# The scan's backward chain dealt out over the steps on GpSimd, and both norm-weight rows spread ahead of the transposes

## The chip, the cores and the metric

The kernel runs on one core of a Trainium2 chip. A core has TensorE (matmuls, PE in the profile; its weight loads are listed as PEld), VectorE (DVE), ScalarE (ACT), GpSimd (POOL) and SyncE (SP). The engines run side by side, each through its own queue of instructions in a fixed order, and wait for each other by semaphores. DMA transfers are issued here from the queues of SP and ACT. The metric is the device time of one execution in microseconds (us).

## What is computed

The reference is one layer of a hybrid encoder on a sequence of 1024 tokens with 1024 channels. Cut to what matters here:

```
h = rmsnorm(x, norm_mix)
proj = h @ w_in                       # q, k, v, z, x/B/C, dt and gates
ssd:  x, B, C = silu(conv(xbc));  dt = softplus(dt_raw + bias)
      y = scan_forward(x, dt, B, C) + scan_backward(x, dt, B, C) + d_skip * x
      y = group_rmsnorm(y * silu(z))
merged = gate_a * (attention @ w_a) + gate_b * (ssd @ w_s)
x = x + merged @ w_out;  x = x + cross_attention(rmsnorm(x), rmsnorm(mem));  x = x + mlp(rmsnorm(x))
```

Both scans go by chunks of 128 tokens, eight in all. Within a chunk a product with a masked decay matrix gives the local part; between chunks a state is carried along: `state[c+1] = decay[c] * state[c] + contribution[c]` forward, and the same from the last chunk to the first backward. The output of chunk c adds `C` times the states that enter the chunk from either side.

## The kernel before

Matmuls of the big projections are done as three products of split numbers (high by high, high by low, low by high), which is why weights are split after loading: ScalarE copies the high part (L66), GpSimd subtracts it for the low part (L69, tile `wlo`).

**The start (`phase0`).** Two 128-row tiles of `mem` and eight of `x` are normalised. Their norm weights come as one row each (`gr`), and TensorE spreads a row over 128 partitions by products with a column of ones into PSUM (tile `gb`, two halves of 512 columns, L225 and L228). `norm_rows` takes the sum of squares on ScalarE (L131), the power on GpSimd (L124) and scales on VectorE (L143). `mem_split` transposes a tile on TensorE (L191, tile `nt`) and copies it to `mT` on ScalarE (L192). In the order of TensorE, the row for `mem` is spread first, then the first tile of `mem` is transposed, then one half of the row for `x` is spread, then the second tile is transposed, then the other half. After that come the key and value products of `mem` (`kx_unit`, L203, tile `kxp`; `vx_unit`), alternating with the transposes of the `x` tiles.

**The scan (`ssd_phase`).** Channels form eight groups. TensorE works through jobs that are written out by hand, in which every unit is three matmuls: for a group two convolution jobs (`conv_job`), a gate job, two more convolution jobs and a job for `z`. Between units, small pieces of the scan are put at given places: the eight `state` pieces of a group lie in its `z` job, and the eight `step` pieces of the group before lie in the first four jobs of the next, from step 7 down to step 0, two in a job of 16 units.

- `state(q, c)` makes the contribution of chunk c (TensorE, tile `st`), carries the forward state on VectorE (L511, L512) and puts the contribution to the backward state into `prev[:, c-1, 1]` by ScalarE (L514).
- `back(q)` carries the backward state on GpSimd: six links from chunk 6 down to 1, each a product with the decay into a tile `cb_t` (L520) and an addition into `prev[:, c-1, 1]` (L521). Before, it is called once, at the end of the group's `z` job. `cb_t` shares the two buffers `p1` with a tile of the steps.
- `prep(q, c)` loads cumulative decays for chunk c (`rows`, two DMAs issued on ACT's queue, L528), GpSimd masks them (L529 and L531, the triangle of either direction), ScalarE takes eight exponentials (L538, L539, tiles `ef` and `eb`), and VectorE adds the two (L540).
- `mask(q, c)` multiplies `ef` with the product of B and C (L545 on TensorE, L547 on VectorE).
- `step(q, c)` calls `mask` for chunk c-1 and `prep` for chunk c-2, then does the local products (L561, into `cb`) and the product of C with the entering states `prev[:, c]` (L565, tile `yo`). VectorE scales `yo` into `t` (L569). GpSimd makes the skip term `p1` (shown as `p`, L573) and adds the backward part of `t` (L575). VectorE sums up into `yz` (L577 to L579), ScalarE squares (L580).
- `conv_post` follows a convolution job: a first pass on ScalarE (L379), four on VectorE (L383, L385), a tanh (L387) and a last one on VectorE (L388).

TensorE's order is that of the program. The other engines' orders, and the slots of buffers, are made at build time by a list scheduler, which goes by the place of an instruction in the program and by its own estimate of when the inputs are there. A piece can so be moved ahead of its place: `prep`'s loads and masks run up to three steps early where the buffers allow it. `tc.issue_after(ins)` keeps what is traced inside it behind `ins` on the engine of `ins`.

## Time and profile before

| | |
|---|---|
| median of 3 runs | 2375.82 us (2375.48 to 2376.95) |
| profiled execution | 2374.8 us, its span 2373.0 us |
| TensorE busy | 2328.3 us (98%) |
| VectorE busy | 1567.7 us (66%) |
| ScalarE busy | 1124.2 us (47%) |
| GpSimd busy | 865.4 us (36%), 827 instructions |
| scan, by the steps | about 151 to 935 us of the span |

A row of the timeline gives the start and the length in us, the engine, the line, the operation, the output and input tiles with their shapes, how many instructions are merged in the row, and in brackets how long the engine was idle before and what ended that. "ACTq" is a queue of DMA issues. A row of waits gives who waited for whom, the total in us, how many times, and the longest. A row of one line's instructions gives minimum, median and maximum in nanoseconds and the first and last start. In the row of a stretch stand its bounds, its length and the busy time and count of PE, PEld, DVE, ACT and POOL, then the granted clock, the DMA share and the data rate.

### The profile page before, as it was taken

How to read it: one execution, taken by the hardware profiler on the slowest of the kernel's cores; microseconds unless marked ns; L12 is line 12 of the kernel's file. 1: busy time of each engine (PE TensorE's matmuls, PEld its weight loads, DVE VectorE, ACT ScalarE, POOL GpSimd, SP SyncE). 2: the span in 40 equal slices, each digit the busy share in tenths (PEclk: the TensorE clock that was granted, in tenths of full speed). 3: DMA queues.
4: the chain of work that ended last, by engine and by line, in shares of the span. 5: the costliest groups of instructions: out<-in, count | busy, mean ns of one | idle time of the engine just before them, and what ended most of it. 6: DMA issues, size and time to landing. Idle time of an engine off the chain costs nothing.

```text
span 2373.0 us, 32192 instructions
## 1 busy us (share of the span) xinstructions
PE 2328.3 (98%) x11812; PEld 1930.2 (81%) x11812; DVE 1567.7 (66%) x2523; ACT 1124.2 (47%) x2398; POOL 865.4 (36%) x827
## 2 busy tenths in 40 slices
PE   9999999999999999999999999999999999999998
PEld 7888888888888887877777888888987887788887
DVE  4757566565756654375658987975685456689984
ACT  4445545555554555387765543345543333234341
POOL 2244536263443625255541013305475444200010
PEclk9999999999999999999999999999999999999999
DMA  6223323232322323111116247203253345722301
GB/s 219 84 77 98 87 83 115 72 107 68 111 78 92 107 75 104 45 36 54 39 52 228 101 151 266 89 1 98 98 173 125 110 135 175 281 94 77 128 27 71
DMA packets 150033, 251.01 MB, mean 106 GB/s; under 512 B 11250, under 2 KB 86130, under 8 KB 149876
## 3 DMA queue, kind: packets, MB, share of 16 engines
q1 hardware_dynamic: 79264, 210.67, 26.3%
q10 hardware_dynamic: 70612, 38.29, 5.7%
q8 instruction: 93, 1.52, 0.3%
q14 instruction: 64, 0.52, 0.1%
HBM read 201.47 MB, written 47.45 MB: 105 GB/s over the span
## 4 chain that ended last, share of the span: by engine, by line
PE 70%; DVE 12%; POOL 7%; ACT 5%; issue 4%; DMA 2%; POOLq 0%; ACTq 0%; SPq 0%; DVEq 0%
PE dps L1482 10%; PE mps L1482 8%; PE pb L1277 5%; PE pc L1277 3%; PE zp L89 3%; PE zp L85 2%; PE zp L90 2%; PE cps L90 2%; PE cps L85 2%; PE cps L89 2%; PE st L506 2%; POOL prev L521 2%; DVE cx L385 1%; PE mps L85 1%; POOL cb_t L520 1%
## 5 line engine op out<-in xcount | busy, mean ns | idle before, releaser
L69 POOL TENSOR_TENSOR wlo<-raw,whi 128x1024 fp32r<-128x1024 f32 x104 | 255.0, 2453 | 471.9 <-ACT whi L66 459.1
L1433 ACT ACTIVATE kt<-row 128x512 fp32r<-128x512 f32 x264 | 144.0, 620 | 185.8 <-PE dps L1482 83.2
L1482 PE MATMUL mps<-kt 128*128 128x512 f32 x1008 | 230.5, 390 | 1.5 <-DVE kt L1434 1.5
L1482 PE MATMUL dps<-kt 128*128 128x512 f32 x1008 | 228.6, 389 | 0.0
L1482 PEld LDWEIGHTS mps<-kt 128*128 128x128 f32 x1008 | 188.7, 188 | 42.1 <-DVE kt L1434 3.1
L1482 PEld LDWEIGHTS dps<-kt 128*128 128x128 f32 x1008 | 189.2, 188 | 39.3
L85 PE MATMUL cps<-kt,whi 128*128 128x512 f32 x512 | 215.0, 420 | 0.0
L66 ACT ACTIVATE whi<-raw 128x1024 fp32r<-128x1024 f32 x104 | 109.6, 1055 | 203.5 <-DMA raw<-in_wa_dram 42.7
L90 PE MATMUL cps<-kt,wlo 128*128 128x512 f32 x512 | 200.0, 391 | 0.0
L89 PE MATMUL cps<-kt,whi 128*128 128x512 f32 x512 | 199.4, 389 | 0.0
L1434 DVE TENSOR_TENSOR kt<-row,kt 128x512 fp32r<-128x512 f32 x264 | 171.9, 698 | 4.1 <-ACT kt L1433 4.0
L124 POOL TENSOR_TENSOR rr<-rv,mhalf 128x1 f32<-128x1 f32 (+1 forms) x50 | 35.0, 701 | 239.4 <-DVE rv L122 237.6
L529 POOL TENSOR_SCALAR_AFFINE_SELECT rows<-rows 128x512 f32<-128x512 f32 x64 | 44.2, 691 | 202.5 <-DMA rows<-d_cs 201.6
L1223 POOL TENSOR_TENSOR wop<-w,wop 128x512 fp32r<-128x512 f32 x64 | 86.0, 1347 | 85.8 <-ACT wop L1222 79.9
L89 PEld LDWEIGHTS cps<-kt,whi 128*128 128x128 f32 x512 | 96.3, 188 | 25.4 <-issue 6.7
L85 PEld LDWEIGHTS cps<-kt,whi 128*128 128x128 f32 x512 | 96.2, 188 | 25.1 <-issue 6.7
L90 PEld LDWEIGHTS cps<-kt,wlo 128*128 128x128 f32 x512 | 96.1, 188 | 20.7
L85 PE MATMUL gps<-kt,whi 128*128 128x512 f32 x240 | 102.2, 426 | 0.0
L539 ACT ACTIVATE eb<-rows,ebias 128x128 f32<-128x128 f32 x256 | 89.1, 392 | 23.3 <-POOL rows L531 23.3
L719 DVE CUSTOM_DVE_ANT_0 t<-sps,bias 128x384 f32<-128x384 f32 (+1 forms) x128 | 64.4, 522 | 51.6 <-PE sps L718 49.6
L730 POOL TENSOR_SCALAR t<-t,den 128x384 f32<-128x384 f32 (+1 forms) x128 | 69.2, 560 | 80.3 <-DVE den L728 70.8
L538 ACT ACTIVATE ef<-rows,ebias 128x128 f32<-128x128 f32 x256 | 90.1, 391 | 14.7 <-PE cb L561 14.7
(372 smaller groups left out, 6387.6 us busy)
## 6 DMA issues: line engine op xcount, KB each, us to landing
rows<-d_cs ACTq DMA_DIRECT2D x128, 256.0 KB, 3.8
raw<-in_wssd_dram SPq DMA_DIRECT2D x48, 512.0 KB, 3.6
raw<-in_wup_dram SPq DMA_DIRECT2D x40, 512.0 KB, 3.8
d_u<-c SPq DMA_DIRECT2D x64, 256.0 KB, 2.6
row<-in_wdn_dram SPq DMA_DIRECT2D x28, 512.0 KB, 6.6
row<-d_u SPq DMA_DIRECT2D x28, 512.0 KB, 6.6
x<-in_x_dram SPq DMA_DIRECT2D x16, 512.0 KB, 6.2
raw<-in_wg_dram SPq DMA_DIRECT2D x16, 512.0 KB, 3.5
```

The costliest lines, as they stand in the source:

```text
L66: steps = [nc.scalar.activation(hi, raw, AF.Copy)]
L69: steps.append((eng or nc.gpsimd).tensor_tensor(lo, raw, hi.bitcast(F32), ALU.subtract))
L85: i = mm(out, l[0], r[0], start=first, stop=False)
L89: mm(out, l[0], r[1], start=False, stop=False)
L90: mm(out, l[1], r[0], start=False, stop=last)
L538: A.activation(ef[:, h], rows[:, 0, h], AF.Exp, bias=kx.ebias[:, b, j, 0, o:o + 1])
L539: A.activation(eb[:, h], rows[:, 1, h], AF.Exp, bias=kx.ebias[:, b, j, 1, o:o + 1])
L1223: self.kx.nc.gpsimd.tensor_tensor(t[:, 1], src, t[:, 0].bitcast(F32), ALU.subtract)
L1277: self.kx.nc.tensor.matmul(ps, w[:, i, ks], act[:, k, j], start=start and k == 0 and m == 0, stop=k == 3 and m == 2, skip_group_check=True)
L1433: nc.scalar.activation(t[:, j, 0], src, AF.Copy)
L1434: nc.vector.tensor_tensor(t[:, j, 1], src, t[:, j, 0].bitcast(F32), ALU.subtract)
L1482: self.kx.nc.tensor.matmul(ps[t], lt[:, k, x, ts], rt[:, k, y], start=n in (1, 2, 5) and k == 0 and m == 0, stop=k == 3 and m == 2, skip_g ...
```

## The change

All four products that spread the norm weights now come ahead of the first transpose. `back` becomes a function of one link, is no longer called at the end of the `z` job, and is called in step c (from 7 down to 2) for link c-1, behind the second mask of that step's `prep` (chunk c-2). Its tile `cb_t` gets a buffer of its own.

```diff
         gb = [psum_g(kx, "gb") for _ in range(2)]
-        for h in range(2):
-            PE.matmul(gb[0][:, h * 512:(h + 1) * 512], ones, gr[:, 0, h * 512:(h + 1) * 512], start=True, stop=True)
+        for i in range(2):
+            for h in range(2):
+                PE.matmul(gb[i][:, h * 512:(h + 1) * 512], ones, gr[:, i, h * 512:(h + 1) * 512], start=True, stop=True)
         for j in range(2):
             mem_split(rows(xm[j], gb[0]), j * P)
-            PE.matmul(gb[1][:, j * 512:(j + 1) * 512], ones, gr[:, 1, j * 512:(j + 1) * 512], start=True, stop=True)
...
-        def back(q):
+        def back(q, c):
             prev = q.prev
-            for c in range(NT - 2, 0, -1):
-                t = sp.tile([P, 256], F32, tag="p1", bufs=2, name="cb_t")
-                G.tensor_tensor(heads(t), heads(prev[:, c, 1]), decay(q, 1, c), ALU.mult)
-                G.tensor_tensor(prev[:, c - 1, 1], prev[:, c - 1, 1], t, ALU.add)
+            t = sp.tile([P, 256], F32, tag="cbt", bufs=1, name="cb_t")
+            G.tensor_tensor(heads(t), heads(prev[:, c, 1]), decay(q, 1, c), ALU.mult)
+            G.tensor_tensor(prev[:, c - 1, 1], prev[:, c - 1, 1], t, ALU.add)
...
-            G.affine_select(out=rows[:, 1], in_=rows[:, 1], compare_op=ALU.is_ge, fill=NEG, base=0,
-                            pattern=[[0, 4], [-1, P]], channel_multiplier=1)
+            q.shut = G.affine_select(out=rows[:, 1], in_=rows[:, 1], compare_op=ALU.is_ge, fill=NEG, base=0,
+                                     pattern=[[0, 4], [-1, P]], channel_multiplier=1)
...
             if d1 - d0 == 2:
                 G.tensor_tensor(p1, p1, t[:, 1], ALU.add)
+            if c > 1:
+                with tc.issue_after(q.shut.ins):
+                    back(q, c - 1)
...
-            at[64] += [(prep, q, 6), (back, q), (mask, q, 7)]
+            at[64] += [(prep, q, 6), (mask, q, 7)]
```

## The prediction

> **What bounds the kernel now.** I read the page first (busy shares), then the waits of TensorE, then TensorE's timeline at the places where it waits, and last the timelines of GpSimd, ScalarE and VectorE ahead of these places.

> ```profile
> span 2373.0 us, 32192 instructions
> PE 2328.3 (98%) x11812; PEld 1930.2 (81%) x11812; DVE 1567.7 (66%) x2523; ACT 1124.2 (47%) x2398; POOL 865.4 (36%) x827
> ```

> TensorE is busy for 98% and the change takes no matmul away, so it can only win out of TensorE's 44.7 us of idle time. Where that is, and who ends it, stands in the waits of TensorE:

> ```profile
> PE yo L565 <- DVE t L569: 6.7, 10, 1.0
> ...
> PE nt L191 <- DVE xn L143: 2.0, 1, 2.0
> ...
> PE cb L561 <- DVE ef L547: 1.4, 1, 1.4
> ```

> The first and third lie in the scan's steps, the second at the start: the two places that the diff touches. The first is larger than the view says, because TensorE's ends are modelled and waits under about a quarter microsecond aren't listed. Starts tell it better. In an undisturbed step, `yo` starts 0.84 us after the first `cb` product:

> ```profile
> 397.23 1.00 PE L561 MATMUL cb<-xtok,ef 128*128 128x64 f32 x8
> 398.07 1.08 PE L565 MATMUL yo<-prev,cC 128*128 128x512 f32 x2
> ```

> The same distance in three other steps, the first and the last late one before the tail and one between:

> ```profile
> 170.81 1.00 PE L561 MATMUL cb<-xtok,ef 128*128 128x64 f32 x8
> 171.91 1.10 PE L565 MATMUL yo<-prev,cC 128*128 128x512 f32 x2
> ...
> 389.21 1.00 PE L561 MATMUL cb<-xtok,ef 128*128 128x64 f32 x8
> 390.59 1.10 PE L565 MATMUL yo<-prev,cC 128*128 128x512 f32 x2 [0.38 <-DVE t L569]
> ...
> 822.62 1.00 PE L561 MATMUL cb<-xtok,ef 128*128 128x64 f32 x8
> 823.69 1.10 PE L565 MATMUL yo<-prev,cC 128*128 128x512 f32 x2
> ```

> They are 1.10, 1.38 and 1.07 us: losses of 0.26, 0.54 and 0.23. Taken over all 64 steps this way, 21 are late, three in each of seven groups (steps 5, 4 and 2), by 0.21 to 1.12 us, together 11.2 us. So 6.7 is the lower and 11.2 the upper figure for this wait; I take 11.2, since starts aren't modelled.

> **Why `yo` waits for `t`.** In the group around 361 to 410 us, GpSimd and then the two engines behind it:

> ```profile
> 361.91 2.40 POOL L69 TENSOR_TENSOR wlo<-raw,whi 128x1024 fp32r<-128x1024 f32 x1 [0.49 <-ACT whi L66]
> 364.28 0.61 POOL L520 TENSOR_TENSOR cb_t<-prev,dec 128x256 f32<-128x256 f32 x1
> ...
> 373.26 0.61 POOL L573 TENSOR_TENSOR p<-xtok,dsk 128x256 f32<-128x256 f32 x1
> 373.83 0.73 POOL L521 TENSOR_TENSOR prev<-prev,cb_t 128x256 f32<-128x256 f32 x1
> ...
> 375.27 0.82 POOL L529 TENSOR_SCALAR_AFFINE_SELECT rows<-rows 128x512 f32<-128x512 f32 x1
> ...
> 377.80 0.63 POOL L531 TENSOR_SCALAR_AFFINE_SELECT rows<-rows 128x512 f32<-128x512 f32 x1
> ```

> ```profile
> 369.41 0.93 ACTq L528 DMA_DIRECT2D rows<-d_cs  x2
> 378.46 0.99 ACT L539 ACTIVATE eb<-rows,ebias 128x128 f32<-128x128 f32 x3 [0.47 <-POOL rows L531]
> 379.36 1.19 ACT L379 ACTIVATE cx<-cps,cols 128x1024 f32<-128x1024 f32 x1
> ...
> 380.58 1.28 DVE L383 SCALAR_TENSOR_TENSOR cx<-cps,cols,cx 128x1023 f32<-128x1023 f32 x1 [4.39 <-ACT cx L379]
> ...
> 389.77 0.68 DVE L569 TENSOR_TENSOR t<-yo,ecs 128x512 f32<-128x512 f32 x1
> ```

> The reader is to see one chain. The backward chain holds GpSimd from 364.28 to 374.56. The two pairs of masks that follow run at 375.27 to 378.43. ScalarE's exponentials wait for them, and the convolution's first pass (`cx`, L379) stands behind these in ScalarE's order and starts at 379.36. VectorE waits 4.39 us for it, with `t` of step 6 behind it in its own order, and is late from there: `t` of step 5 ends at 390.45, and `yo` of step 4 starts at 390.59, right after.

> **The change, part one: the chain dealt out.** The 48 links (six in each of eight groups, two instructions each) stay, with the durations of these rows:

> ```profile
> L521 POOL TENSOR_TENSOR prev<-prev,cb_t x48: 722/738/1271, 154.3 to 895.6; 128x256 f32<-128x256 f32 x48
> L520 POOL TENSOR_TENSOR cb_t<-prev,dec x48: 611/622/635, 153.6 to 894.4; 128x256 f32<-128x256 f32 x48
> rows<-d_cs ACTq DMA_DIRECT2D x128, 256.0 KB, 3.8
> ```

> A link is 0.62 + 0.74 = 1.36 us of GpSimd, and no DMA is issued by it. It moves past `p` (L573, L575) of its own step, past the masks of the step's `prep`, and past the splits of weights (L69) that come due between. The order behind a mask on the same engine adds no wait of its own. The link of step c writes `prev` for step c-2, so it has two step distances, and even one (398.07 - 390.59 = 7.48 us) is the length of five links. So TensorE doesn't wait for links. What stands behind a link on GpSimd (`p`, a split, the next masks) is late by at most 1.36 us, which the idle third of GpSimd covers; without that cover it is 1.36 us in a step.

> What comes earlier: the second pair of rows is issued at 369.41 and lands 3.8 us later, at 373.2. Two masks of 0.63 us end at 374.5, where they ended at 378.43. The four exponentials behind them take 1.28 us, so `cx` can start at 375.8 in place of 379.36: 3.5 us earlier (its own input is complete at about 374). All that follows on VectorE moves with it, and the largest loss at a `yo` is 1.12 us. So I let all 21 losses go: **-11.2 us** (bounds: 0 if VectorE is late for another reason, -11.2 if all go). What is late next in the step is `t` itself, waiting for its `yo`, which is the right order. The new tile for `cb_t` costs nothing in time: it takes the link's result out of the pair of buffers that `p` uses, so one wait fewer is possible.

> The third wait lies in the last group, where steps follow closer:

> ```profile
> 921.45 2.40 POOL L69 TENSOR_TENSOR wlo<-raw,whi 128x1024 fp32r<-128x1024 f32 x1 [3.04 <-ACT whi L66]
> 921.58 2.55 DVE L578 TENSOR_TENSOR yz<-yz,p 128x256 f32<-128x256 f32 x1
> 925.34 1.08 PE L561 MATMUL cb<-xtok,ef 128*128 128x64 f32 x8 [1.37 <-DVE ef L547]
> 380.50:409.70 29.20, 28.58 (x138) 22.78 (x137) 27.34 (x37) 18.21 (x46) 19.45 (x20) 1.00 0.43 127
> ```

> A VectorE addition that is done in 0.42 us elsewhere takes 2.55 us here, just as long as GpSimd's split beside it, and the mask product behind it is late by that. Whether both meet again is chance: between 0 and -1.37 I take half, **-0.7 us**.

> **Part two: both rows of norm weights first.** TensorE's start, with the engines that feed it:

> ```profile
> 2.79 3.75 PE L225 MATMUL gb<-gr,ones 1*128 1x512 f32 x4 [2.79 <-DMA gr<-in_gmem_dram]
> 7.17 2.47 DVE L143 SCALAR_TENSOR_TENSOR xn<-x,rr,gb 128x1024 f32<-128x1024 f32 x2
> 8.51 1.97 PE L191 MATMUL nt<-ident,xn 128*128 128x128 f32 x8 [1.98 <-DVE xn L143]
> 10.41 2.07 PE L228 MATMUL gb<-gr,ones 1*128 1x512 f32 x2
> ...
> 14.41 0.60 ACT L192 ACTIVATE mT<-nt 128x512 f32<-128x512 f32 x1 [0.26 <-PE nt L191]
> 16.31 5.81 PE L203 MATMUL kxp<-mT,w 128*128 128x256 f32 x16
> 22.82 3.62 PE L203 MATMUL kxp<-mT,w 128*128 128x256 f32 x16
> ```

> The second row's two halves (2.0 us each, 10.41 to 12.41) now follow at 6.54 and end at 10.54. The two sets of transposes (1.9 us each) have their inputs at 8.4 and 9.6 and end at 14.34, and `kxp` starts there in place of 16.31: **-1.97 us**, the idle time filled. The second half of `mT` is copied 0.7 us after the last transpose and is wanted by the fifth of eight products, so it should not delay; if it does, the gain is 1.3. From there on TensorE runs on with small gaps, so the gain is carried.

> These matmuls run slowly: the first `kxp` takes 5.81 us, the next 3.62. The rate changes within the first `kxp`, after 8 us or more without a gap. If the fast rate comes at the same instant as before, the earlier `kxp` runs slow throughout; at half rate, an estimate from these two rows, that is 2 x 3.62 = 7.24 us, 1.43 more than now, and the gain is 0.5. If the fast rate is there from its first product, the gain is 1.97 + 2.19 = 4.2. I take 1.97, the case in which the rate changes as long after the first `kxp` product as now.

> [...]

> **Sum.** 11.2 + 0.7 + 1.97 = 13.9 us. The profiled execution took 2374.8 us (its span 2373.0 and 1.8 around it), so it would take 2360.9; the median of the runs is 2375.82, 1.0 above that execution, and would be **2362**. A difference under 0.2% (4.75 us) can't be told from no change here.

> **The rivals.**

> *Half the losses stay* (links now lie among VectorE's work): 5.6 + 2.0 = 7.6, 2368.2. For it: links beside VectorE's additions lengthen them. Against: 3.5 us earlier is three times the worst loss.

> *The jam has another cause, only the start is won*: 2375.8 - 2.0 = 2373.8, no measurable change. For it: VectorE is busy 27.34 of 29.20 us in the late stretch (the last row above: stretch, its length, then busy times of PE, PEld, DVE, ACT and POOL), so it may be late by its own load. Against: it idles 4.39 us just ahead of that stretch.

> *Fast matmuls from the start*: transposes and second row in half their 7.8 us, `kxp` as the second one: 1.97 + 3.9 + 2.2 = 8.1 at the start, with 11.9 from the scan, 2355.8. Against it stands the slow stretch just shown.

> *Links block VectorE: slower.* Its place is the late stretch, where four of the six links now fall: up to 4 x 1.36 = 5.4 us of blocking, as in the row of 2.55 us, against 29.20 - 27.34 = 1.86 us to spare. If `cx` comes no earlier, TensorE loses 3.6 us more in each of seven groups: +25 - 2 = +23, 2399. It makes the kernel measurably slower from (4.75 + 1.97) / 7 = 1.0 us more per group, that is, from 2.8 us blocked. Against it: `cx` comes 3.5 us earlier, which alone covers the 3.6.

> [...]

> **How the numbers follow.** The forecast 0.58 (its own range 2359 to 2367, from 6.7 at the `yo` and half of the start's gain to all of the tail's 1.37 and 4.2 at the start); half the losses stay 0.10; fast from the start 0.04; only the start 0.20; slower 0.08. Faster 0.58 + 0.10 + 0.04 = 0.72, same 0.20, slower 0.08. The range leaves out the slower case and the fast start: 2359 to 2374.

> **What would show it.** Right: masks of step 5's neighbours at 369 to 375 us in that group, not behind a chain of 10 us; `cx` (L379) within 2 us of its matmuls' end; `yo` 0.84 us after `cb` in steps 5, 4 and 2; no wait of `nt` at the start, `kxp` near 14.3. Wrong: `t` still ahead of a late `yo` though `cx` is early (VectorE's load or blocked additions), links queued before masks, a `yo` that waits for `prev`, or a split of weights that TensorE waits for.

## The result and the profile after

The changed kernel takes 2357.12 us (median of 6 runs, 2356.42 to 2361.01) beside 2375.27 us of the kernel before (6 runs): ratio 0.9927 [0.9914, 0.994], so 18.2 us won. The forecast was 2362, 13.9 won, and its range began at 2359. The sign held; the gain was larger than every case in the range. The profiled execution took 2356.88 us. Its page:

```profile
span 2355.1 us, 32190 instructions
PE 2323.0 (99%) x11812; PEld 1928.8 (82%) x11812; DVE 1570.3 (67%) x2523; ACT 1124.4 (48%) x2398; POOL 872.9 (37%) x827
```

TensorE's idle time went from 44.7 to 32.1 us, and its busy time fell by 5.3 us with the same number of matmuls. The idle time is what the waits gave back; the busy time is in part a higher rate at the start, shown below (2.05 us at the first `kxp`). In the view of TensorE's waits (who waits for whom, total us, times, longest), `yo` is gone, and of the waits of `nt` at the start the one at L191:

```profile
PE gb L226 <- DMA gr<-in_gmem_dram: 2.9, 1, 2.9
...
PE nt L152 <- DVE xn L143: 1.1, 1, 1.1
```

**The scan.** The same group as before the change, now some 10 us earlier. GpSimd first:

```profile
360.75 0.73 POOL L528 TENSOR_SCALAR_AFFINE_SELECT rows<-rows 128x512 f32<-128x512 f32 x1 [2.12 <-DMA rows<-d_cs]
361.44 0.81 POOL L530 TENSOR_SCALAR_AFFINE_SELECT rows<-rows 128x512 f32<-128x512 f32 x1
362.22 0.79 POOL L519 TENSOR_TENSOR cb_t<-prev,dec 128x256 f32<-128x256 f32 x1
...
364.24 0.63 POOL L528 TENSOR_SCALAR_AFFINE_SELECT rows<-rows 128x512 f32<-128x512 f32 x1
365.36 0.63 POOL L530 TENSOR_SCALAR_AFFINE_SELECT rows<-rows 128x512 f32<-128x512 f32 x1 [0.49 <-DMA rows<-d_cs]
365.96 0.62 POOL L519 TENSOR_TENSOR cb_t<-prev,dec 128x256 f32<-128x256 f32 x1
```

Then ScalarE, VectorE and TensorE, and VectorE's waits for the convolution's first pass:

```profile
366.02 0.99 ACT L538 ACTIVATE eb<-rows,ebias 128x128 f32<-128x128 f32 x3 [1.78 <-POOL rows L530]
366.92 1.19 ACT L379 ACTIVATE cx<-cps,cols 128x1024 f32<-128x1024 f32 x1
...
368.14 1.28 DVE L383 SCALAR_TENSOR_TENSOR cx<-cps,cols,cx 128x1023 f32<-128x1023 f32 x1 [2.31 <-ACT cx L379]
...
379.83 1.00 PE L560 MATMUL cb<-xtok,ef 128*128 128x64 f32 x8
380.67 1.08 PE L564 MATMUL yo<-prev,cC 128*128 128x512 f32 x2
```

```profile
DVE cx L383 <- ACT cx L379: 22.6, 14, 2.4
```

One link follows each pair of masks, and the second pair waits for its DMA, no longer for the chain. `cx` (L379) starts at 366.92 where it started at 379.36. The step's `yo` in this stretch lies 9.12 us earlier because of what was won ahead of it, so 3.3 us of that is the group's own; VectorE waits 2.31 us for it in place of 4.39. `yo` of step 4 follows `cb` at 0.84 us again. Taken over all 64 steps, the late starts sum to 0.07 us, where they were 11.3.

**The start:**

```profile
2.87 7.16 PE L226 MATMUL gb<-gr,ones 1*128 1x512 f32 x8 [2.87 <-DMA gr<-in_gmem_dram]
9.96 3.67 PE L191 MATMUL nt<-ident,xn 128*128 128x128 f32 x16
14.14 3.76 PE L203 MATMUL kxp<-mT,w 128*128 128x256 f32 x16 [0.50 <-ACT mT L192]
17.73 1.04 PE L152 MATMUL nt<-ident,xn 128*128 128x128 f32 x8
```

`kxp` begins at 14.14 (16.31 before), but it also takes 3.76 us in place of 5.81: the fast rate is there from its first product.

**The account.** Starts of the same `yo` in two profiles give what was won up to there. "Start" is the gain at the first `yo` (157 us before), "scan" what comes on to step 2 of the last group (919 us), "tail" from there to the last `yo` (933 us), "rest" what the span has besides. All against the profiled execution before:

| kernel (labels of the experiments below) | start | scan | tail | rest | span |
|---|---|---|---|---|---|
| changed kernel | 4.43 | 11.71 | 1.43 | 0.33 | 2355.1 |
| changed kernel, again (e9) | 5.10 | 11.71 | 1.63 | 1.66 | 2352.9 |
| start alone (e1) | 2.50 | -0.46 | -0.49 | -0.35 | 2371.8 |
| scan alone (e2) | 0.61 | 11.71 | 1.60 | 2.38 | 2356.7 |
| unbroken transposes (e3) | 0.24 | 11.71 | 1.63 | -1.68 | 2361.1 |
| no idle gap (e4) | 2.60 | 11.71 | 1.63 | -0.64 | 2357.7 |
| full rows (e8) | 1.47 | 11.71 | 1.62 | 0.40 | 2357.8 |
| warm start (e11) | 4.69 | 11.71 | 1.62 | 0.58 | 2354.4 |
| warm, mixed (e12) | 0.25 | 11.71 | 1.62 | 1.52 | 2357.9 |
| bridged wait (e14) | 4.91 | 11.72 | 1.62 | -1.95 | 2356.7 |
| chain kept whole, pass first (e5) | 0.08 | 7.74 | 0.27 | 1.71 | 2363.2 |
| dealt out, no order (e6) | 5.07 | 7.59 | 0.34 | 0.10 | 2359.9 |
| short fills (e10) | 2.27 | 8.03 | 0.62 | 0.48 | 2361.6 |
| long fills (e13) | 5.10 | 1.57 | 0.01 | -3.68 | 2370.0 |
| links twice (e7) | 4.47 | -11.01 | -3.33 | 1.27 | 2381.6 |

The reader is to see how fixed the scan is (11.71 wherever the scan is as changed) and how the start, in the kernels that have the changed kernel's (with e11 and e14), falls into two kinds: 2.27 and 2.50 (e10, e1), and 4.43 to 5.10 in the others. The rest, -3.7 to 2.4 us, differs between kernels that are identical there.

### The profile page after: what moved, and what is told of

Read it like the earlier page. It is cut to its first block, busy times and chain, and to the rows that moved or that the text cites. A ratio compares the mean times of both kernels' runs of the same rounds, so it can differ in the third digit from the quotient of the medians.

```text
span 2355.1 us, 32190 instructions
## 1 busy us (share of the span) xinstructions
PE 2323.0 (99%) x11812; PEld 1928.8 (82%) x11812; DVE 1570.3 (67%) x2523; ACT 1124.4 (48%) x2398; POOL 872.9 (37%) x827
## 3 DMA queue, kind: packets, MB, share of 16 engines
q8 instruction: 93, 1.52, 0.3%
## 4 chain that ended last, share of the span: by engine, by line
PE 80%; DVE 9%; ACT 4%; DMA 3%; issue 2%; POOL 1%; SPq 0%; ACTq 0%; POOLq 0%; DVEq 0%
PE dps L1484 10%; PE mps L1484 8%; PE pb L1279 6%; PE cps L90 5%; PE cps L85 4%; PE cps L89 4%; PE pc L1279 3%; PE zp L89 3%; PE zp L90 3%; PE zp L85 3%; PE cb L560 2%; PE yo L564 2%; PE st L506 2%; PE gps L85 2%; PE gps L89 2%
## 5 line engine op out<-in xcount | busy, mean ns | idle before, releaser
L69 POOL TENSOR_TENSOR wlo<-raw,whi 128x1024 fp32r<-128x1024 f32 x104 | 255.4, 2456 | 413.8 <-ACT whi L66 400.0
L66 ACT ACTIVATE whi<-raw 128x1024 fp32r<-128x1024 f32 x104 | 109.7, 1056 | 209.2 <-PE cps L89 43.4
L528 POOL TENSOR_SCALAR_AFFINE_SELECT rows<-rows 128x512 f32<-128x512 f32 x64 | 42.7, 667 | 211.4 <-DMA rows<-d_cs 205.8
## 6 DMA issues: line engine op xcount, KB each, us to landing
rows<-d_cs ACTq DMA_DIRECT2D x128, 256.0 KB, 3.9
d_u<-c SPq DMA_DIRECT2D x64, 256.0 KB, 2.3
```

The source lines that it names most:

```text
L66: steps = [nc.scalar.activation(hi, raw, AF.Copy)]
L69: steps.append((eng or nc.gpsimd).tensor_tensor(lo, raw, hi.bitcast(F32), ALU.subtract))
```

## The experiments

**Half by half.** e1 has the start of the changed kernel and the chain of the kernel before; e2 the reverse.

```diff
# e1_start_only, against the changed kernel
-            if c > 1:
-                with tc.issue_after(q.shut.ins):
-                    back(q, c - 1)
...
-            at[64] += [(prep, q, 6), (mask, q, 7)]
+            at[64] += [(prep, q, 6), (back, q), (mask, q, 7)]
# e2_scan_only, against the changed kernel
-        for i in range(2):
-            for h in range(2):
-                PE.matmul(gb[i][:, h * 512:(h + 1) * 512], ones, gr[:, i, h * 512:(h + 1) * 512], start=True, stop=True)
+        for h in range(2):
+            PE.matmul(gb[0][:, h * 512:(h + 1) * 512], ones, gr[:, 0, h * 512:(h + 1) * 512], start=True, stop=True)
         for j in range(2):
             mem_split(rows(xm[j], gb[0]), j * P)
+            PE.matmul(gb[1][:, j * 512:(j + 1) * 512], ones, gr[:, 1, j * 512:(j + 1) * 512], start=True, stop=True)
```

> The kernel before with the second part of the change alone (both rows of norm weights spread ahead of the transposes); the chain on GpSimd stays whole at the end of the z job. By the traces of before and after, the first transposes of x start at 21.9 and 17.7 us, so this part alone should give 4.2 to 4.4 us (2371), and the losses at yo in the steps (11.2 us) stay. If the fast rate came by chance in the one profile looked at, the gain is nearer 2.0 (2373) and differs from execution to execution.

> The first part alone: links dealt out behind the masks, the start as in the kernel before. Should give 11.7 us in the seven groups and 1.4 in the tail, 13.1 together (2362), with yo 0.84 us after the first cb product in all steps, and the first transposes of x at 21.9 us again. If both parts lean on each other, the two gains don't add up to the 18.2 measured for both.

e1: 2373.95 us, ratio 0.999 [0.9981, 0.9999], 3.1 us won. e2: 2361.1 us, ratio 0.9935 [0.9922, 0.9949], 16.0 us won. The scan carries most, and the two add up to about the whole (19.1 against 18.2). In e1 TensorE's start went differently from the changed kernel with the same instructions:

```profile
9.70 3.67 PE L191 MATMUL nt<-ident,xn 128*128 128x128 f32 x16
13.88 5.90 PE L203 MATMUL kxp<-mT,w 128*128 128x256 f32 x16 [0.50 <-ACT mT L192]
19.61 1.04 PE L152 MATMUL nt<-ident,xn 128*128 128x128 f32 x8
```

`kxp` takes 5.90 us, and the first transposes of `x` start 1.9 us later than the changed kernel's (19.61, 17.73). So the start's gain has a sure part, 2.3 to 2.5 us (e1, e10), and a part that depends on when TensorE's rate doubles. The next runs are about that moment.

**What sets the moment at the start.** e3 keeps the 16 transposes of `mem` in one piece between the two rows; e4 fills the idle time with one half of the second row and leaves the other half between the transposes. Both keep the scan of the changed kernel.

```diff
# e3_unbroken: order of TensorE at the start
+        spread(0, 0); spread(0, 1)
         for j in range(2):
             mem_split(rows(xm[j], gb[0]), j * P)
+        spread(1, 0); spread(1, 1)
# e4_no_gap
+        spread(0, 0); spread(0, 1); spread(1, 0)
+        mem_split(rows(xm[0], gb[0]), 0)
+        spread(1, 1)
+        mem_split(rows(xm[1], gb[0]), P)
```

> The changed kernel, but the second row of norm weights is spread behind both sets of transposes: the idle stretch of 2 us ahead of the transposes is back, while the 16 transposes follow each other without the one-row products between. Theory A (the fast rate comes after some 3.5 to 4.5 us of unbroken products with 128 rows; one-row products don't count): the second row's products or at the latest the kxp products are fast, the first transposes of x start at 18 to 18.5 us. Theory B (what counts is the time since the last idle stretch, 11 to 12 us of any products): all stays slow to about 20 us, first transposes of x at 22 us.

> The changed kernel, but half of the second row is spread ahead of the first transposes and the other half between the two sets: hardly any idle time is left at the start, but the transposes are parted by one-row products again. Theory A: the first kxp starts near 14.2 us and is slow for some 4 us, taking 5.8 us; first transposes of x at 20 us. Theory B: fast at 14 us as in the changed kernel, first transposes of x at 17.8 us.

e3 took 2362.84 us and e4 2359.45 (one run each). TensorE in e3, then in e4:

```profile
8.47 3.67 PE L191 MATMUL nt<-ident,xn 128*128 128x128 f32 x16 [2.49 <-DVE xn L143]
12.07 3.78 PE L225 MATMUL gb<-gr,ones 1*128 1x512 f32 x4
15.78 6.39 PE L203 MATMUL kxp<-mT,w 128*128 128x256 f32 x16
```

```profile
12.35 1.97 PE L191 MATMUL nt<-ident,xn 128*128 128x128 f32 x8
14.16 5.56 PE L203 MATMUL kxp<-mT,w 128*128 128x256 f32 x16
```

In e4 the idle time ahead of the transposes shrinks to 0.77 us (8.45), there is none from there on, and `kxp` is still slow: closing the gap is not what brings the rate. With 3.62 us for 16 products at the later rate (0.23 each) and twice that at the earlier one (in the kernel before, the first product of `kxp` starts at 16.31 and the fifth at 18.17, 0.46 apart), 5.56 us means a change about 3.9 us after the first product, an estimate from these rows. In e3, 16 transposes without a break (3.67 us) were not enough: `gb` behind them is slow, and so is `kxp` for 5.5 us. The strict form of the theory, by which such a stretch suffices, missed.

e8 makes the norm weights' rows into full tiles of 128 rows, zero but for the first, and the column of ones likewise, so the same sums come from products with 128 rows:

```diff
-        ones = p0.tile([1, P], F32, name="ones")
-        gr = p0.tile([1, 2, D], F32, name="gr")
+        ones = p0.tile([P, P], F32, name="ones")
+        gr = p0.tile([P, 2, D], F32, name="gr")
```

> The changed kernel, but the products that spread the norm weights run over 128 rows (127 of them zero) in place of one; two fills of a tile come ahead, and the row's load waits for them by about 1 to 2 us. In the traces so far the rate doubled 3.2 to 5.4 us after the first kxp product in five kernels, and in the changed kernel already behind the transposes, 4 us after the first of them. [...] Theory B2 (the moment depends on the time since the start or on kxp's kind of product, not on the rows): slow as before up to 14 us or more.

```profile
7.00 6.25 PE L229 MATMUL gb<-gr,ones 128*128 128x512 f32 x8 [7.00 <-DMA gr<-in_gmem_dram]
13.08 1.91 PE L191 MATMUL nt<-ident,xn 128*128 128x128 f32 x16
16.37 3.72 PE L203 MATMUL kxp<-mT,w 128*128 128x256 f32 x16 [1.38 <-ACT mT L192]
```

2359.61 us (one run). The row of weights came late (7.00 us, 4.1 later than in the changed kernel, where 1 to 2 had been expected), and `kxp` with it (16.37), so the time itself says little. But the rate doubles inside the eight products (6.25 us, where eight one-row products take 7.16), and the 16 transposes behind them take 1.91 us in place of 3.67. Work with all 128 rows brought the fast rate here, within 6.25 us; 7.16 us of one-row products had not.

The changed kernel was run again (e9), and two kernels tried to bring the rate in earlier: e11 with 16 transposes of the identity ahead of the four products, e12 with 12 ahead and two more ahead of each product. Nobody reads what they write.

```diff
# e11_warm
+        hot = kx.pp.tile([P, 512], F32, tag="p", name="hot")
+        for j in range(16):
+            PE.transpose(hot[:, (j % 4) * P:(j % 4 + 1) * P], kx.ident, kx.ident)
# e12_warm_mix: 12 ahead, and
         for i in range(2):
             for h in range(2):
+                warm(2)
```

> The changed kernel once more, beside runs of the kernel before. Theory (start gain is 2.3 us sure and about 2.2 us that come or not with the moment at which TensorE's rate doubles; scan gain 11.7 us and the tail 1.4): 2357 to 2361 us, 16 to 19 us ahead. In the profile the scan's 21 late starts of yo are gone again (sum under 1 us), the first kxp starts at 13.5 to 14.5 us and takes either 3.7 us (early rate) or 5.5 to 6 us (late rate). Rival (the early rate belongs to the order of the four products): 3.7 us again, the first transposes of x at 17 to 18 us.

> The changed kernel with 16 transposes of the identity (128x128) ahead of the four products that spread the norm weights. Nobody reads them. Theory (TensorE's rate doubles after some 3 to 5 us of work with all 128 rows; one-row products don't count): the transposes take 16 x 0.23 = 3.7 us from about 1 us on and hide the wait for the row of weights (2.8 us) for the most part; the spread starts at 4 to 5 us at the slow rate, where the rate doubles only later; kxp at 15 to 16 us but surely with 3.7 us; sum 0 to +1.5 us against the changed kernel, 2358 to 2360. Rival (any work counts, once 3 to 5 us of it went by without a gap): the rate doubles within the spread, its 7.5 us become 4 to 5, the transposes take 1 us each set, kxp starts at 10.5 to 12 us, 2353 to 2356.

> The changed kernel with 12 transposes of the identity ahead of the spread and two more ahead of each of its four products, so that work with 128 rows never stops for long. Theory (128-row work makes the rate double): the rate doubles within the first two products of the spread, the others and the transposes of mem run at twice the rate, kxp starts at 11 to 13 us and takes 3.7 us: 1 to 3 us ahead of the changed kernel, 2354 to 2357. Rival (a one-row product sets the rate back, however short): everything up to kxp stays slow and the 20 transposes come on top: kxp at 17 to 18.5 us, 2360 to 2362.

Beside runs of the kernel before (2376.91 us): e9 2356.96, ratio 0.9912 [0.9898, 0.9927]; e11 2358.47, 0.9919 [0.9904, 0.9934]; e12 2359.9, 0.9925 [0.9908, 0.9941]. Nothing separates the three by time. TensorE's start in e11, then e12:

```profile
1.35 3.68 PE L226 MATMUL hot<-ident 128*128 128x128 f32 x16 [1.35 <-POOL ident L52]
4.96 3.92 PE L229 MATMUL gb<-gr,ones 1*128 1x512 f32 x8
9.47 3.31 PE L191 MATMUL nt<-ident,xn 128*128 128x128 f32 x16 [0.60 <-DVE xn L143]
13.65 3.72 PE L203 MATMUL kxp<-mT,w 128*128 128x256 f32 x16 [0.86 <-ACT mT L192]
```

```profile
13.96 0.69 PE L228 MATMUL hot<-ident 128*128 128x128 f32 x2
14.44 3.62 PE L191 MATMUL nt<-ident,xn 128*128 128x128 f32 x16
17.89 4.14 PE L203 MATMUL kxp<-mT,w 128*128 128x256 f32 x16
```

In e11 the rate doubles behind 16 transposes (3.68 us), as many as had not been enough in e3: the eight one-row products take 3.92 us. Behind them it is lost again, as 16 transposes take 3.31 us, where in e8 they took 1.91; the one-row products and the wait of 0.60 us lie between, and which of them lost it isn't separated. The 3.2 us won at the spread bring nothing, since the transposes must wait for VectorE's `xn` (0.60 us) and `kxp` for ScalarE's copy (0.86): the normalisation sets the time from there, and both expectations missed `kxp`'s start (13.65). In e12 the rate stays slow up to `kxp`, although some 9 us of 128-row work went before (2.82, four times 0.69, 3.62); the rival's place for `kxp` (17 to 18.5) was right. With one-row products between, the rate had not doubled; whether each of them sets it back, as the rival has it, or they only thin the work out isn't separated.

e14 puts three transposes of the identity into the 0.5 us in which TensorE waits for `mT`:

```diff
+        for j in range(3):
+            PE.transpose(hot[:, j * P:(j + 1) * P], kx.ident, kx.ident)
```

> The changed kernel with three transposes of the identity between the transposes of mem and the first kxp product, in the 0.5 us in which TensorE waits for mT. Nobody reads them. Theory (the rate doubles 3 to 5.7 us after the start of an unbroken stretch of 128-row work, and the 0.5 us wait breaks the stretch where it has not doubled by then): the moment lies 3 to 5.7 us after the first transpose of mem, so the first transposes of x start at 17.0 to 19.2 us with kxp starting at 13.6 to 14.5; 2356 to 2359 us. Rival (so short a wait breaks nothing and the moment is free up to 8.6 us behind the first transpose, as in the kernel with the start alone): it can still come 4 us or more behind the first kxp product, the first transposes of x at 19.6 to 20 us, kxp taking 5.7 to 6 us; 2357 to 2361 us.

2356.09 us, ratio 0.9914 [0.9901, 0.9928], the first transposes of `x` at 17.21: as the theory said, but the rival allows it too. Where one-row products part the work, the doubling comes 2.9 (e11, in the transposes of `mem`) to 5.7 us (e4) into the last unbroken stretch of 128-row work. In the changed kernel that stretch begins at the transposes of `mem`, which last 3.67 us and are followed by the wait of 0.5. Of seven executions with this start, `kxp` was fast almost from its beginning in five (changed kernel, e6, e7, e9, e13); in two (e1, e10) the moment came 4.6 and 4.2 us after that product, 8.7 and 8.3 us into the stretch, as if the stretch had begun anew behind the wait. That the wait does this is not shown, and the changed kernel speaks against it: its `kxp` takes 3.76 us where the other four take 3.72, so its rate seems to have doubled inside the first product, just behind that wait and 4.2 us after the first transpose. What decides between the two kinds stays open.

**Is it the chain's length or the order behind it?** e5 leaves the start and the chain as before but for a buffer of its own for `cb_t`, and puts the exponentials of chunks 3 and 2 behind the convolution's first pass on ScalarE.

```diff
-    A.activation(acc, ps, AF.Identity, bias=kx.cb[:, j:j + 1], scale=cw(2))
+    kx.pass0 = A.activation(acc, ps, AF.Identity, bias=kx.cb[:, j:j + 1], scale=cw(2))
...
-                t = sp.tile([P, 256], F32, tag="p1", bufs=2, name="cb_t")
+                t = sp.tile([P, 256], F32, tag="cbt", bufs=1, name="cb_t")
...
-            with tc.issue_after(q.zt[8 - c].ins) if c > 4 else ExitStack():
+            with tc.issue_after(q.zt[8 - c].ins if c > 4 else kx.pass0.ins) if c > 4 or c in (2, 3) else ExitStack():
```

> The kernel before with the chain whole at its old place and the old start. Changed are two orders: cb_t has a buffer of its own (so p stands ahead of the chain on GpSimd), and the exponentials of chunks 3 and 2 stand behind the convolution's first pass on ScalarE, where they stood ahead of it. Theory 1 (TensorE's losses at yo come from VectorE, which waits for that pass behind exponentials behind masks behind the chain): the pass starts within 2 us of its matmuls' end and at least 8 of the 11.3 us at yo go, with the chain still there: 2366. Theory 2 (the 10 us of links on GpSimd themselves are the trouble): the losses stay, 2376.

2366.3 us, ratio 0.9953 [0.994, 0.9965]. Two rows of its waits, of VectorE and of TensorE:

```profile
DVE cx L383 <- ACT cx L379: 10.0, 7, 1.4
DVE yz L578 <- POOL p L575: 65.6, 44, 4.5
```

```profile
PE cb L561 <- DVE ef L547: 2.3, 5, 1.1
```

With `cx` out of the queue behind the masks the late `yo` fall from 11.3 to 1.4 us, as the first theory had it, and 7.74 of the 11.71 us come back with the chain still in one piece. This is not the order's own share, since the buffer of `cb_t` changed too (see e6). The other 4 us stay away: TensorE waits 2.3 us for the mask products, whose exponentials are now the later ones. VectorE's wait for `p` is hardly longer than it was, 65.6 us beside 64.1 in two rows of the kernel before:

```profile
DVE yz L578 <- POOL p L575: 34.7, 32, 3.6
DVE yz L578 <- POOL p L573: 29.4, 8, 5.5
```

e6 deals the chain out, but without the order behind the masks:

```diff
-                with tc.issue_after(q.shut.ins):
-                    back(q, c - 1)
+                back(q, c - 1)
```

> The changed kernel without the rule that keeps a link behind the step's masks: the links are traced one per step, but nothing holds them back, and the list scheduler draws all six together again, ahead of the two late pairs of masks; p stays ahead of them. Theory 1: the masks are late as before, the pass starts some 3 us later than in the changed kernel, and most of the 11.3 us of losses are back: 2368 to 2371. Theory 2 (dealing them out over the steps of the program or cb_t's own buffer is what helps): stays at 2358 to 2361.

2361.64 us, ratio 0.9931 [0.9917, 0.9944]. The scheduler puts all six links of a group together again, ahead of the two late pairs of masks. GpSimd in the group shown above, and two rows of waits:

```profile
366.59 0.73 POOL L520 TENSOR_TENSOR prev<-prev,cb_t 128x256 f32<-128x256 f32 x1
367.28 0.64 POOL L528 TENSOR_SCALAR_AFFINE_SELECT rows<-rows 128x512 f32<-128x512 f32 x1
```

```profile
DVE cx L383 <- ACT cx L379: 38.7, 14, 4.7
...
PE yo L564 <- DVE t L568: 2.7, 3, 1.2
```

VectorE's wait for `cx` is back (38.7 us, before the change 38.3), and yet the late `yo` come to 3.9 us in place of 11.3. The first theory missed: the time lies just above the range of the second. What that theory named, `cb_t`'s own buffer, can be seen in GpSimd's order. In the kernel before, where `cb_t` shares the buffers of `p`, three `p` (L573) stand between the chain's first link and the last mask, two of them as follows; in e6 there is one, at 368.47:

```profile
374.64 0.68 POOL L573 TENSOR_TENSOR p<-xtok,dsk 128x256 f32<-128x256 f32 x1
...
376.65 0.61 POOL L573 TENSOR_TENSOR p<-xtok,dsk 128x256 f32<-128x256 f32 x1
```

```profile
368.47 0.61 POOL L572 TENSOR_TENSOR p<-xtok,dsk 128x256 f32<-128x256 f32 x1
...
369.62 0.64 POOL L530 TENSOR_SCALAR_AFFINE_SELECT rows<-rows 128x512 f32<-128x512 f32 x1
```

From the first link to the end of the last mask this makes 14.15 us before (364.28 to 378.43) and 12.94 in e6 (357.32 to 370.26), in all seven groups alike, so `cx` comes about 1.2 us earlier though the chain is as long as before. e5 has the same order there, and the buffer is the one edit that both share. So it seems to carry most of e6's 7.59 us and an unknown part of e5's 7.74; no run changes it alone, and its exact share stays open. What the links behind the masks add to e6 is 4.1 us of the scan and 1.1 of the tail.

**Is GpSimd's cover really there?** The prediction costed the moved links at nothing. e7 doubles each link (the copy goes to a tile that nobody reads); e10 and e13 add a write of constants per link instead, which reads no operand; e13's was sized after the second link of e7.

```diff
# e7_links_twice
+            more = sp.tile([P, 256], F32, tag="more", bufs=1, name="more")
+            G.tensor_tensor(heads(more), heads(prev[:, c, 1]), decay(q, 1, c), ALU.mult)
+            G.tensor_tensor(more, prev[:, c - 1, 1], more, ALU.add)
# e10_links_fill (1024) and e13_fill_long (1504)
+            more = sp.tile([P, 1504], F32, tag="more", bufs=1, name="more")
+            G.memset(more, 0.0)
```

> The changed kernel with the work of each link done twice on GpSimd, the first time into a tile that nobody reads: 48 x 1.36 = 65 us more of GpSimd. If links behind the masks are covered by idle GpSimd and don't hold up VectorE, the time stays within 2 us of the changed kernel (2358 to 2361). If blocked VectorE additions reach TensorE, as in the slower rival, each link costs up to 1.36 us there: from +5 to +50 us.

> The changed kernel with each link followed by a write of 128x1024 constants into a tile that nobody reads, an estimate of 1.0 to 1.4 us of GpSimd per link (from the 0.2 us of the 128x128 one at the start), as much as the second link in the kernel with doubled links, but with no operand read. Theory Q (the 24 us of the doubled links came from GpSimd's queue: masks, p and splits late by 1.36 us each): the same here, 2375 to 2385 us, yo late by about 1.6 us at step 2 of each group. Theory V (they came from VectorE, shut out while GpSimd reads its operands): within 5 us of the changed kernel, 2357 to 2363, VectorE's busy time within 3 us of 1570 where the doubled links had 1580, and late starts of yo under 3 us in sum.

> The changed kernel with a write of 128x1504 constants per link, sized from the 0.956 us of the 128x1024 write and the 0.205 us of the 128x128 one (0.84 ns an element of the row): 1.36 us, exactly what the second link took in the kernel with doubled links, and no operand read. Theory Q (GpSimd's queue alone makes the 24 us): the scan loses as much as with the doubled links, its steps and tail gaining nothing against the kernel before: 2372 to 2385 us. Theory V (most of it comes from VectorE while GpSimd reads): the scan keeps at least half of its gain, as with the shorter write (8.7 us kept of 13.3): 2359 to 2366 us, VectorE busy within 5 us of 1570.

e7 took 2383.51 us, ratio 1.0026 [1.0015, 1.0037]; e10 2363.74, 0.994 [0.9925, 0.9956]; e13 2372.94, 0.9984 [0.9975, 0.9992]. Busy times of e7, then a row of GpSimd's groups of e13 (busy us, mean ns) and what TensorE and VectorE wait for in it:

```profile
PE 2334.0 (98%) x11812; PEld 1935.9 (81%) x11812; DVE 1579.9 (66%) x2523; ACT 1124.0 (47%) x2398; POOL 934.2 (39%) x923
```

```profile
L520 POOL MEMSET more<- 128x1504 f32 x48 | 65.1, 1355 | 0.0
...
PE yo L566 <- DVE t L570: 7.6, 7, 1.3
...
DVE yz L582 <- POOL p L576: 47.7, 39, 3.6
```

In e13 the writes take 1.36 us each, as planned, and the scan loses 10.1 of its 11.71 us, mostly at one late `yo` per group. VectorE is not busier (1568.5 us); it waits for `p` longer (47.7 us, 36.8 in the changed kernel). So theory V missed: GpSimd's queue by itself takes nearly the whole gain. It isn't all of e7 either, which loses 22.7 with nearly the same GpSimd time (934.2 against 928.7) and has VectorE busy 1579.9 us, 9.6 more than in the changed kernel. Theory Q missed that part. The pair isn't quite even: e7's second link takes 1.54 us on average (0.66 and 0.88), so some of the difference may be queue. e10, at 2363.74 us, lay just above V's range and far below Q's. The loss is steep: 38 us more GpSimd work (e10) cost the scan 3.7 us, 56 us more (e13) cost 10.1.

In the pair e7 and e13 VectorE's busy time grew with the doubled links, which read operands (1579.9 us), and not with the writes (1568.5 us; 1570.3 in the changed kernel). In the changed kernel's profile one addition into `yz` takes 0.94 us beside that of a link (883.74, L580), where the median of its line is 0.43.

## Why the prediction was right in part and short in size

Against the profiled execution the sum was 4.0 us short (2360.9 forecast, 2356.9 measured): 2.5 at the start, 0.7 in the tail, 0.5 in the scan, 0.3 behind it. The other 0.8 us of the median's miss are a difference: the first median lay 1.0 us above its profiled execution, the second 0.2.

- **The chain, -11.2.** Right in size: 11.71 in every profile with this scan, all 21 late `yo` gone, with `cx` 3.3 us earlier (3.5 forecast). Taking starts rather than the 6.7 us of the waits view was the better choice. What it was laid to is right only in part. The path (masks, exponentials, `cx`, VectorE, `t`) stands, but not only the chain made the masks late: so did the `p` between, and the new tile that moved them had been put at nothing ("costs nothing in time"). With the chain still whole, e6 brings 7.59 of the 11.71; what the links' new places add to that is 4.1.
- **Links at no cost.** Right for the size they have. VectorE's and GpSimd's busy time in the late stretch (columns as in the prediction's row of a stretch):

```profile
371.36:400.58 29.22, 29.22 (x144) 23.54 (x143) 25.05 (x34) 16.75 (x40) 23.83 (x24) 1.00 0.45 137
```

  GpSimd has 23.83 us of work there (19.45 before) and VectorE 25.05 for 34 instructions (27.34 for 37 before), 0.74 us each in both: on average the links there did not lengthen its instructions. But the cover was thinner than "the idle third of GpSimd" suggests; e10 and e13 show it ending within another microsecond per link. What counts, by VectorE's longer wait for `p` in e13, is the room between a mask and the `p` that VectorE needs, not the share of the span.
- **The tail, -0.7.** The step that failed is "whether both meet again is chance". The two do meet again, as before (GpSimd's split beside the first row runs from 903.88 for 2.40 us), and the loss is gone all the same:

```profile
904.01 2.54 DVE L580 TENSOR_TENSOR yz<-yz,p 128x256 f32<-128x256 f32 x1
...
906.93 0.68 DVE L546 TENSOR_TENSOR ef<-ef,cb 128x512 f32<-128x512 f32 x1
...
907.76 1.08 PE L560 MATMUL cb<-xtok,ef 128*128 128x64 f32 x8
```

  This addition came at 921.58 before, so it moved by 17.57 us, while TensorE's last steps ahead of it (to 919 us before) had moved by 16.14. VectorE's whole chain is 1.43 us earlier against TensorE, and the mask product ends at 907.61, just ahead of `cb`. The term should have been the full 1.37 (1.43 to 1.63 in the runs); why VectorE came earlier there isn't traced.
- **The start, -1.97.** This is the term that was mis-sized: 4.43 in the profile. 2.17 us of it are `kxp`'s earlier start (14.14, forecast 14.34), near the forecast by two errors that cancel: TensorE waits 0.50 us for `mT`, which the sum did not have, and the pieces run faster together than apart (7.16 us for the whole spread, where its parts took 3.75, 2.07 and 2.07). Another 2.05 are the fast rate from `kxp`'s first product, which stood in the text as the bound of 4.2. What failed is the choice between the bounds: "the rate changes as long after the first `kxp` product as now". In e4 and e12, with one-row products between the transposes, the rate was still slow at the start of `kxp` (14.16 and 17.89 us); with 16 transposes in one piece the doubling came 4.2 us after the first of them. That is the more frequent of two kinds: in e1 and e10, with the same start, the rate changed as late as the prediction assumed, and the term came to 2.50 and 2.27. The row for the early kind was there before the change (`kxp` slow after 8 us without a gap, of which two pieces were one-row products), read only as evidence against fast matmuls from the start.
- **The range.** Its lower end was the sum of the favourable bounds: 4.2 + 1.37 + 11.2 = 16.8, 2359.0. All three came in at or above their bound (4.43, 1.43, 11.71), with 0.3 besides: 17.9. Bounds taken from single rows were treated as limits; each was only a good estimate.
- **The rivals.** Half the losses stay, and only the start won: refuted by the late `yo` and by e2. Fast from the start: half true, the spread and the transposes stay slow (7.16 and 3.67 us), `kxp` is fast (3.76). Links block VectorE: not at this size (0.74 us per instruction in the late stretch, before and after); doubled links do lose (e7, 6.1 us slower than the kernel before), but e13 shows GpSimd's queue as the larger part of that.

None of the variants beats the changed kernel by more than the intervals tell (e14's median is 0.9 us below e9's, in other runs).

## What to carry to other kernels

When TensorE is busy for 98%, look for who is last in a queue that TensorE's supplier shares: here a chain on GpSimd, with `p` behind it, held masks, these held ScalarE's exponentials, and these a convolution pass that had nothing to do with them. Look at shared buffers as well as at lengths: with the chain still whole, a buffer of its own for one tile seems to have brought most of 7.6 us. Dealing the chain out needs its order fixed, since the list scheduler gathered it again (e6), and it pays only as long as the engine has room at those places (e10, e13). Where several favourable bounds add up in a forecast, let the range reach beyond their sum.

## What the runs showed of the hardware beyond that

```profile
14.00:18.00 4.00, 4.00 (x8) 1.92 (x7) 1.34 (x2) 1.79 (x4) 0.11 (x1) 1.00 1.00 401
```

- Kernels with the same instructions at the start fall into two kinds (first transposes of `x` at 17.1 to 17.7 us or 19.6 to 19.9), about 2 us apart by `kxp`'s length (5.7 and 5.9 us, 3.7 to 3.8), beside a spread of 4.6 over the changed kernel's runs. Both profiles of the changed kernel itself are of the early kind.
- GpSimd's writes of constants without operands cost 0.84 ns per element of a row (0.205 us at 128 columns, 0.956 at 1024, 1.355 at 1504), and left VectorE's busy time where it was (1567.8 and 1568.5 us, 1570.3 in the changed kernel).
